# One attention kernel, four edits: shared reciprocals, norms and low parts on GpSimd, one copy

## The chip, the cores and the metric

The kernel runs on one core of a Trainium2 chip. The metric is the device time of one launch in microseconds (us). Before the change it is 1409.32 us, the median of three runs (1409.03 to 1409.68). The engines are called as in the profile: PE is TensorE, DVE is VectorE, ACT is ScalarE, POOL is GpSimd, SP is SyncE.

## The reference: what is computed

A two-layer decoder trunk over 512 tokens of width 1024, all in float32. Layer 0 mixes by retention and an mLSTM; layer 1 by sparse attention. Each layer then has a gated MLP with a short convolution and adds a gated per-layer embedding. The change touches layer 1's mixer alone:

```
z = rms_norm(h) @ w_in                      # q (16 heads x 64), six k/v parts, 48 gates
q = rms_norm(q per head) * 1/8              # 2 groups of 8 heads
kc, vc = compress(k), compress(v)           # 31 blocks: gelu(blk @ w1) @ w2; kc is normed
o_cmp = softmax(q kc) vc                    # compressed branch
o_slc = softmax(q ks) vs                    # "selected": all 8 blocks are selected, so causal
o_win = softmax(q kw) vw                    # window of 512 = all tokens, so causal
o = g0*o_cmp + g1*o_slc + g2*o_win ; y = o @ w_out
```

The two causal branches (here 0 and 1) share the query and differ in keys, values and gate.

## The kernel before

Every float32 product is made of three matmuls: each operand is split in a high part (rounded by ACT, `split` L133) and a low part (the rest, L134), and `mm3` (L150 to L154) adds high x high, high x low and low x high. A weight tile of 128x1024 is fetched, split and kept in one of three buffers by `load` (L136). Which engine makes the low part, DVE or POOL, is told by `lo_seq`, a string that `load` turns round by one letter at each call; `nsa_mixer` (L615) sets it to "v" (DVE) at L951, to "g" (POOL) at L990 and to "v" again at L1050.

Instructions are not issued in the order of the program text. A planner (the Tile framework) sets each engine's order before the run, from priorities and its own costs; loads get a priority 500 instructions ahead of their place. On the chip each engine then goes through its list strictly in order and waits on semaphores.

Layer 1 has two stages of interest.

*The run-up* (about 650 to 770 us). `thin` makes the compressed-branch inputs and gates, `kv` projects keys and values (four tiles of weights), `kv_evac` and `key_stack` norm and transpose them, `hidden` runs the two compressing MLPs (four tiles of w1 each, 32 short matmuls), `q0` and `q1` project the queries of the two groups (four tiles each). These are 22 loads. `q_copy` takes the queries out of PSUM, `q_norm` (L814) norms the first group's four token tiles in two calls: squares L818, sums of squares L819, an inverse root by small instructions L183 to L188, the scaling L825, the split L830 and L831. `q_stack` (L835) transposes. `cmp_keys_t` (L790) transposes the compressed keys' two halves into one PSUM bank, and after each of the two an ACT copy (L795) takes it out. `cmp_scores` and `cmp_probs` make the compressed branch's softmax.

*The loop* (about 770 to 970 us). It has 96 steps: 16 heads times six units in `UNITS` (L34). A unit is a query tile j and one or both branches: (3, branch 0), (3, branch 1), (1, both), (2, branch 0), (2, branch 1), (0, both). `scores` (L887) of a step makes the scores in PSUM (L894 to L896), their negated maximum on DVE (L897), exponentials with row sums on ACT (L899), the reciprocal of the sums on DVE (L900), and on POOL the product of exponentials, reciprocal and gate (L902). Four steps later (`LAG`) `probs` transposes the result on PE (L914) and splits it (L133, L134); `values` (L918) multiplies by the values (L936). The second group's preparation is hung in by step number (`START`, L35, and `hooks`): the embedding's projection from step 1, the second group's `q_norm` at steps 14 and 21, its `q_stack` at 28, 32, 36 and 40, the first group's `cmp_probs` at step 0, the second's `cmp_scores` at 42. `load` uses POOL in this stage: seven tiles.

Of the kernel before, what the change touches and what calls it, by code (L numbers as in the profile page):

```python
# [10 lines left out]
F32 = mybir.dt.float32  # L11
# [3 lines left out]
AF = mybir.ActivationFunctionType  # L15
ALU = mybir.AluOpType
# [3 lines left out]
P = 128  # L20
# [11 lines left out]
WARM = 10  # L32
LAG, VALUES_LAG = 4, 2
UNITS = ((3, (0,)), (3, (1,)), (1, (0, 1)), (2, (0,)), (2, (1,)), (0, (0, 1)))  # L34
START = {"embed": (1, 1), "q_norm": (14, 7), "q_stack": (28, 4), "cmp_scores": 42, "cmp_probs": 47, "fetch": 51, "out": (60, 2)}  # L35
BANKS = {"a": 4, "b": 3, "o": 1}
AHEAD = 500

# [22 lines left out]
class Trunk:  # L61
# [553 lines left out]
    def nsa_mixer(self):  # L615
        nc, I, tc = self.nc, self.I, self.tc
# [3 lines left out]
        with ExitStack() as ctx:  # L620
            np_ = ctx.enter_context(tc.tile_pool(name="nsa", bufs=1))
# [17 lines left out]
            n = self.norm_in(C_NSA)  # L639
            gate = np_.tile([P, NTT, 16, 3], F32, name="gate")  # L640
            kc = np_.tile([P, 2, 64], F32R, name="kc")
# [94 lines left out]
            def hidden(which, xs):  # L736
                ph = self.ps("b")
                for c in range(4):
                    hi, lo = self.load(I["w1"][which, c])
                    for q in range(4):  # L740
                        jj = 4 * c + q
                        ws = slice(256 * q, 256 * q + 256)
                        x = xs[c // 2][:, jj % 8]
                        if jj:
                            nc.tensor.matmul(ph[0:64, 0:256], x[:, 0], lo[:, ws], start=False, stop=False)
                        nc.tensor.matmul(ph[:, 0:256], x.rearrange("p a s -> p (a s)"), hi[:, ws], start=jj == 0, stop=jj == 15)
                        if jj == 0:
                            nc.tensor.matmul(ph[0:64, 0:256], x[:, 0], lo[:, ws], start=False, stop=False)
                hid = self.sc()
                nc.scalar.activation(hid[0:64, 0:256], ph[64:128, 0:256], AF.Copy)  # L750
                nc.vector.tensor_tensor(hid[0:64, 0:256], hid[0:64, 0:256], ph[0:64, 0:256], ALU.add)
                nc.scalar.activation(hid[0:64, 0:256], hid[0:64, 0:256], AF.Gelu_apprx_tanh)
                return hid
# [36 lines left out]
            def cmp_keys_t(st):  # L790
                pk = self.ps("b")
                for a in range(2):
                    src = st[:, 1 - a : 3 - a].bitcast(F32).rearrange("p a d -> p (a d)")
                    nc.tensor.transpose(pk[:, 64 * a : 64 * a + 64], src, self.ident[0:64, 0:64])
                    nc.scalar.activation(kc[:, a], pk[:, 64 * a : 64 * a + 64], AF.Copy)  # L795


            def cmp_values(po):
# [9 lines left out]
            def q_copy(ps, t0):  # L808
                both = self.slot(2 + t0 // 2)
                for i in range(2):  # L810
                    nc.scalar.activation(both[:, i], ps[i], AF.Copy, scale=n.r[:, t0 + i : t0 + i + 1])
                return both

            def q_norm(both, sts):  # L814
                ss = self.small(16)
                for i in range(2):
                    sq = self.sc()
                    nc.vector.tensor_tensor(sq, both[:, i], both[:, i], ALU.mult)  # L818
                    nc.vector.tensor_reduce(ss[:, 8 * i : 8 * i + 8], sq.rearrange("p (h d) -> p h d", h=8), AX, ALU.add)  # L819
                nc.vector.tensor_scalar(ss, ss, 1.0 / 64, EPS, ALU.mult, ALU.add)  # L820
                r = self.rsqrt(ss, 16)
                nc.vector.tensor_scalar(r, r, 0.125, None, ALU.mult)
                for i in range(2):
                    z = both[:, i].rearrange("p (h d) -> p h d", h=8)
                    nc.vector.tensor_tensor(z, z, r[:, 8 * i : 8 * i + 8].unsqueeze(2).to_broadcast([P, 8, 64]), ALU.mult)  # L825
                    halves = []
                    for c in range(2):
                        st = self.y().rearrange("p (h a d) -> p h a d", h=4, a=2)
                        zc = z[:, 4 * c : 4 * c + 4]
                        nc.scalar.activation(st[:, :, 0], zc, AF.Copy)  # L830
                        nc.vector.tensor_tensor(st[:, :, 1], zc, st[:, :, 0].bitcast(F32), ALU.subtract)  # L831
                        halves.append(st)
                    sts.append(halves)
# [40 lines left out]
            def cmp_probs(es):  # L874
                pc = []
                for b in range(2):
                    pt = self.ps("b")
                    for j in range(NTT):
                        c0 = 256 * (j % 2) + P * b
                        nc.tensor.transpose(pt[:, j * P : (j + 1) * P], es[j // 2][:, c0 : c0 + P], self.ident)  # L880
                    hi, lo = self.y(), self.y()
                    self.split(hi, lo, pt)
                    pc.append((hi, lo))
                return pc


            def scores(hd, j, bs):  # L887
                g, nb = hd // 8, len(bs)
                w = (j + 1) * P
                qt, br = qs[hd][:, j * P : w], slice(bs[0], bs[-1] + 1)  # L890
                nmx, sm = [np_.tile([P, nb], F32, name=self.nm("sm"), tag=f"sm{nb}", bufs=4) for _ in range(2)]
                pr = np_.tile([P, T], F32, name=self.nm("pr"), tag="pr", bufs=6)[:, 0 : nb * w].rearrange("p (b s) -> p b s", b=nb)
                s = self.ps("a")[:, 0 : nb * w].rearrange("p (b s) -> p b s", b=nb)
                nc.tensor.matmul(s, qt, kst[0][g][:, br, 0:w], start=True, stop=False)  # L894
                nc.tensor.matmul(s, qt, kst[1][g][:, br, 0:w], start=False, stop=False)  # L895
                nc.tensor.matmul(s[:, :, j * P : w], identb, maskb.unsqueeze(1).to_broadcast([P, nb, P]), start=False, stop=True)  # L896
                nc.vector.tensor_reduce(nmx, s, AX, ALU.max, negate=True)  # L897
                for b in range(nb):
                    nc.scalar.activation(pr[:, b], s[:, b], AF.Exp, bias=nmx[:, b : b + 1], accum_out=sm[:, b : b + 1])  # L899
                nc.vector.reciprocal(sm, sm)  # L900
                for b in range(nb):
                    nc.gpsimd.tensor_scalar(pr[:, b], pr[:, b], sm[:, b : b + 1], gate[:, j, hd, 1 + bs[b] : 2 + bs[b]], ALU.mult, ALU.mult)  # L902
                return pr

            def probs(hd, j, bs, pr):
# [42 lines left out]
                    outs[g][0].append(hi)  # L948
                    outs[g][1].append(lo)

            self.lo_seq = "v"  # L951
            w2r = self.sc()
            nc.sync.dma_start(w2r[:, 0:256], I["w2"])
            w2 = np_.tile([P, 2, 256], F32R, name="w2")
# [19 lines left out]
            st = cmp_keys(po)  # L974
            sts = []
            zq = [q_copy(q0.ps[0:2], 0), q_copy(q0.ps[2:4], 2)]
            q_norm(zq[0], sts)
            q_norm(zq[1], sts)
            hv = hidden(1, xv)
            q1 = self.Tokens(self, I["w_q"][1], n)  # L980
            q1.steps(0, 2)
# [9 lines left out]
            sts1 = []  # L991
            zq = [q_copy(q1.ps[0:2], 0), q_copy(q1.ps[2:4], 2)]
# [5 lines left out]
            def piece(half, m):  # L998
                return lambda: self.out_piece(I["w_nso"], half, m, *outs[half])
# [3 lines left out]
            def embed(m):  # L1003
                return lambda: emb.step(m)

            def more_q(lo, hi):
                def run():
                    for hd in range(lo, hi):
                        qs.append(q_stack(sts1, hd))
                return run  # L1010

            def set_probs(g):
                def run():
                    pcs[g] = cmp_probs(ess[g])
                return run
# [4 lines left out]
            hooks = {}  # L1020

            def at(key, fs):
                first, step = START[key]
                for i, f in enumerate(fs):
                    hooks.setdefault(first + step * i, []).append(f)

            hooks[0] = [set_probs(0)]
            at("embed", [embed(m) for m in range(KD)])
            at("q_stack", [more_q(2 * i, 2 * i + 2) for i in range(4)])
            at("q_norm", [lambda i=i: q_norm(zq[i], sts1) for i in range(2)])  # L1030
            hooks.setdefault(START["cmp_scores"], []).append(set_scores)
            hooks.setdefault(START["cmp_probs"], []).append(set_probs(1))
            hooks.setdefault(START["fetch"], []).append(lambda: self.fetch(self.keep, (0, 2)))
            at("out", [piece(0, m) for m in range(KD)])

            for step in range(len(seq) + LAG + VALUES_LAG + 2):
                if step < len(seq):
                    live[step] = scores(*seq[step])
                if 0 <= step - LAG < len(seq):
                    hd, j, bs = seq[step - LAG]  # L1040
# [231 lines left out]
```

## Time and profile before

| | us |
|---|---|
| median of three runs | 1409.32 |
| the profiled execution's own time | 1410.24 |
| its span, first to last instruction | 1408.5 |
| PE busy | 1378.5 (98%) |
| DVE busy | 852.0 (60%) |
| ACT busy | 640.1 (45%) |
| POOL busy | 349.7 (25%) |
| mean granted TensorE clock | 0.991 |

Busy time is the time in which an engine had an instruction in work. Idle time in brackets behind an instruction is that of its engine just before, with what ended it.

### The profile page before, as it was taken

What the parts mean: (1) busy time and instruction counts of PE and PEld (TensorE: products, weight loads), DVE (VectorE), ACT (ScalarE), POOL (GpSimd) and SP (SyncE); (2) the same over time, 40 slices, a digit from 0 to 9 for tenths busy, and PEclk for the clock granted to TensorE, in tenths of its full rate; (3) what the DMA queues carried; (4) which work ended last, traced back from release to release, by engine and by line L of the source; (5) the groups of instructions that cost most, each with busy time, mean ns of one, the idle gap of its engine ahead of it and who ended that gap; (6) DMA issues with size and microseconds to landing.
All of it is one profiled execution on the core that took longest, in us unless ns stands there. A gap on an engine that the chain in (4) does not pass through costs nothing.

```text
span 1408.5 us, 18029 instructions
## 1 busy us (share of the span) xinstructions
PE 1378.5 (98%) x6726; PEld 1130.2 (80%) x6726; DVE 852.0 (60%) x1419; ACT 640.1 (45%) x1122; POOL 349.7 (25%) x342
## 2 busy tenths in 40 slices
PE   9999999999999999999998989999999999999998
PEld 7778778888888888887787757787888888888887
DVE  6665656565346435566857798777565437534555
ACT  5257426443224313454554777777444224323342
POOL 3465102122041001122112645544222013100120
PEclk9999999999999999999998999999999999999999
DMA  6433323233223332333442100010233323333232
GB/s 216 128 113 95 106 77 111 86 101 103 92 90 105 91 104 83 97 124 95 131 143 63 46 1 31 16 46 17 75 105 105 92 88 105 99 96 96 83 107 75
DMA packets 40031, 127.96 MB, mean 91 GB/s; under 512 B 4740, under 2 KB 5380, under 8 KB 39944
## 3 DMA queue, kind: packets, MB, share of 16 engines
q1 hardware_dynamic: 39656, 126.68, 29.2%
q8 instruction: 53, 0.87, 0.3%
q14 instruction: 34, 0.28, 0.1%
q10 hardware_dynamic: 288, 0.14, 0.0%
HBM read 122.60 MB, written 3.15 MB: 89 GB/s over the span
## 4 chain that ended last, share of the span: by engine, by line
PE 83%; DVE 5%; issue 4%; ACT 3%; POOL 1%; DMA 0%; ACTq 0%; POOLq 0%; DVEq 0%
PE ps L152 25%; PE ps L153 25%; PE ps L154 25%; PE ps L914 2%; PE ps L936 2%; DVE pt L134 1%; DVE sm L897 1%; PE ps L894 1%; ACT pr L899 1%; PE ps L895 1%; PE ps L363 1%; ACT pt L133 1%; ACT wh L133 1%; PE ps L421 1%; POOL acc L200 1%
## 5 line engine op out<-in xcount | busy, mean ns | idle before, releaser
L152 PE MATMUL ps<-y,wh 128*128 128x512 f32 (+1 forms) x1112 | 435.3, 392 | 1.8 <-ACT rb L239 1.1
L153 PE MATMUL ps<-y,wh 128*128 128x512 f32 (+1 forms) x1112 | 432.5, 389 | 0.6 <-POOL y L134 0.6
L154 PE MATMUL ps<-y,wl 128*128 128x512 f32 (+1 forms) x1112 | 432.0, 389 | 0.0
L133 ACT ACTIVATE wh<-wr 128x1024 fp32r<-128x1024 f32 (+2 forms) x223 | 230.2, 1036 | 420.5 <-PE ps L153 347.3
L134 DVE TENSOR_TENSOR wl<-wr,wh 128x1024 fp32r<-128x1024 f32 (+2 forms) x196 | 239.9, 1226 | 43.8 <-ACT wh L133 43.1
L152 PEld LDWEIGHTS ps<-y,wh 128*128 128x128 f32 x1112 | 209.3, 188 | 45.5 <-ACT rb L239 1.3
L154 PEld LDWEIGHTS ps<-y,wl 128*128 128x128 f32 x1112 | 209.3, 188 | 43.5 <-DVE wl L134 0.2
L153 PEld LDWEIGHTS ps<-y,wh 128*128 128x128 f32 x1112 | 209.4, 188 | 43.2 <-POOL y L134 1.1
L1075 POOL TENSOR_TENSOR sc<-sc,rb 128x512 f32<-128x512 f32 x44 | 56.8, 1291 | 476.5 <-ACT sc L1074 476.5
L200 POOL TENSOR_TENSOR acc<-acc,sc 128x512 f32<-128x512 f32 x48 | 73.6, 1534 | 257.9 <-ACT sc L198 255.0
L153 PE MATMUL ps<-gl,wh 128*128 128x512 f32 x352 | 137.1, 389 | 0.0
L154 PE MATMUL ps<-gh,wl 128*128 128x512 f32 x352 | 137.0, 389 | 0.0
L152 PE MATMUL ps<-gh,wh 128*128 128x512 f32 x352 | 137.0, 389 | 0.0
L1090 DVE TENSOR_TENSOR hp<-hp,ps 128x512 f32<-128x512 f32 x48 | 33.0, 688 | 130.4 <-PE ps L154 130.4
L902 POOL TENSOR_SCALAR pr<-pr,sm,gate 128x512 f32<-128x512 f32 (+3 forms) x128 | 79.3, 625 | 85.5 <-DVE sm L900 45.1
L134 POOL TENSOR_TENSOR wl<-wr,wh 128x1024 fp32r<-128x1024 f32 x25 | 61.2, 2451 | 111.0 <-ACT wh L133 103.7
L1076 DVE TENSOR_TENSOR sc<-ps,sc 128x512 f32<-128x512 f32 x44 | 30.4, 692 | 92.4 <-POOL sc L1075 83.2
L1068 DVE TENSOR_TENSOR a<-ps,rb 128x512 f32<-128x512 f32 x44 | 30.4, 690 | 92.1 <-PE ps L154 89.3
L153 PEld LDWEIGHTS ps<-gl,wh 128*128 128x128 f32 x352 | 66.1, 188 | 13.7
L152 PEld LDWEIGHTS ps<-gh,wh 128*128 128x128 f32 x352 | 66.1, 188 | 13.7
L154 PEld LDWEIGHTS ps<-gh,wl 128*128 128x128 f32 x352 | 66.1, 188 | 13.7
L1074 ACT ACTIVATE sc<-sc 128x512 f32<-128x512 f32 x44 | 27.8, 632 | 101.1 <-DVE sc L1073 101.1
(282 smaller groups left out, 2033.0 us busy)
## 6 DMA issues: line engine op xcount, KB each, us to landing
wr<-in_w_up_dram SPq DMA_DIRECT2D x88, 512.0 KB, 3.6
wr<-in_w_down_dram SPq DMA_DIRECT2D x32, 512.0 KB, 3.5
wr<-in_w_plg_dram SPq DMA_DIRECT2D x16, 512.0 KB, 3.6
wr<-in_w_down_dram SPq DMA_DIRECT2D x16, 384.0 KB, 3.1
hp<-in_xT_dram SPq DMA_DIRECT2D x16, 256.0 KB, 4.0
wr<-in_w_abo_dram SPq DMA_DIRECT2D x8, 512.0 KB, 3.7
wr<-in_w_dram SPq DMA_DIRECT2D x8, 512.0 KB, 3.9
wr<-in_w_q_dram SPq DMA_DIRECT2D x8, 512.0 KB, 4.0
```

Source lines behind the costliest of these rows:

```text
L133: self.nc.scalar.activation(hi, src, AF.Copy)
L134: (eng or self.nc.vector).tensor_tensor(lo, src, hi.bitcast(F32), ALU.subtract)
L152: mm(out, ah, bh, start=first, stop=False)
L153: mm(out, ah, bl, start=False, stop=False)
L154: mm(out, al, bh, start=False, stop=last)
L200: eng.tensor_tensor(n.acc, n.acc, sq, ALU.add)
L902: nc.gpsimd.tensor_scalar(pr[:, b], pr[:, b], sm[:, b : b + 1], gate[:, j, hd, 1 + bs[b] : 2 + bs[b]], ALU.mult, ALU.mult)
L914: nc.tensor.transpose(pb[:, i * P : (i + 1) * P], pr[:, n, i * P : (i + 1) * P], self.ident)
L1068: nc.vector.tensor_tensor(a, pa, n.b, ALU.mult)
L1075: nc.gpsimd.tensor_tensor(c, c, n.b, ALU.mult)
L1076: nc.vector.tensor_tensor(c, pb, c, ALU.mult)
L1090: nc.vector.tensor_tensor(self.h[m], self.h[m], ps, ALU.add)
```

## The change

The reciprocals of the row sums: `scores` now keeps one 128x2 tile of sums per head and query tile. Where the two branches are two steps (j = 3 and 2), the second step inverts both sums at once and then issues both POOL products. The maxima get buffers of their own. The squares L818 and scalings L825 of the second group's `q_norm` go from DVE to POOL, at steps 6 and 14 in place of 14 and 21; `q_stack` goes to 20, 26, 32 and 38; the first group's `cmp_probs` to step 3. In the run-up the low parts alternate, DVE and POOL: 11 of the 22 go to POOL. In `cmp_keys_t` one ACT copy follows both transposes.

```diff
-START = {"embed": (1, 1), "q_norm": (14, 7), "q_stack": (28, 4), "cmp_scores": 42, ...}
+START = {"embed": (1, 1), "q_norm": (6, 8), "q_stack": (20, 6), "cmp_scores": 42, ...}
@@ cmp_keys_t
                     nc.tensor.transpose(pk[:, 64 * a : 64 * a + 64], src, self.ident[0:64, 0:64])
-                    nc.scalar.activation(kc[:, a], pk[:, 64 * a : 64 * a + 64], AF.Copy)
+                nc.scalar.activation(kc.rearrange("p a n -> p (a n)"), pk[:, 0:P], AF.Copy)
@@ q_norm
-            def q_norm(both, sts):
+            def q_norm(both, sts, eng):
-                    nc.vector.tensor_tensor(sq, both[:, i], both[:, i], ALU.mult)
+                    eng.tensor_tensor(sq, both[:, i], both[:, i], ALU.mult)
-                    nc.vector.tensor_tensor(z, z, r[:, 8 * i : 8 * i + 8].unsqueeze(2).to_broadcast([P, 8, 64]), ALU.mult)
+                    eng.tensor_tensor(z, z, r[:, 8 * i : 8 * i + 8].unsqueeze(2).to_broadcast([P, 8, 64]), ALU.mult)
@@ scores
+            parts = []
-                nmx, sm = [np_.tile([P, nb], F32, name=self.nm("sm"), tag=f"sm{nb}", bufs=4) for _ in range(2)]
+                nmx = np_.tile([P, nb], F32, name=self.nm("nmx"), tag=f"sm{nb}", bufs=4)
+                if bs[0] == 0:
+                    parts.append([np_.tile([P, 2], F32, name=self.nm("sm"), tag="sums", bufs=4), []])
+                sm, prs = parts[-1]
...
                 for b in range(nb):
-                    nc.scalar.activation(pr[:, b], s[:, b], AF.Exp, bias=nmx[:, b : b + 1], accum_out=sm[:, b : b + 1])
-                nc.vector.reciprocal(sm, sm)
-                for b in range(nb):
-                    nc.gpsimd.tensor_scalar(pr[:, b], pr[:, b], sm[:, b : b + 1], gate[:, j, hd, 1 + bs[b] : 2 + bs[b]], ALU.mult, ALU.mult)
+                    nc.scalar.activation(pr[:, b], s[:, b], AF.Exp, bias=nmx[:, b : b + 1], accum_out=sm[:, bs[b] : bs[b] + 1])
+                    prs.append(pr[:, b])
+                if bs[-1] == 1:
+                    nc.vector.reciprocal(sm, sm)
+                    for b in range(2):
+                        nc.gpsimd.tensor_scalar(prs[b], prs[b], sm[:, b : b + 1], gate[:, j, hd, 1 + b : 2 + b], ALU.mult, ALU.mult)
@@ the run-up's head, the first group's norms, the hooks
-            self.lo_seq = "v"
+            self.lo_seq = "vg"
-            q_norm(zq[0], sts)
-            q_norm(zq[1], sts)
+            q_norm(zq[0], sts, nc.vector)
+            q_norm(zq[1], sts, nc.vector)
-            hooks[0] = [set_probs(0)]
+            hooks[3] = [set_probs(0)]
-            at("q_norm", [lambda i=i: q_norm(zq[i], sts1) for i in range(2)])
+            at("q_norm", [lambda i=i: q_norm(zq[i], sts1, nc.gpsimd) for i in range(2)])
```

## Rows read from the trace of the kernel before

**Rows 1.** Windows: start:end, length, busy us of each engine, granted clock, DMA.
```profile
660.00:740.00 80.00, 78.88 (x397) 64.00 (x398) 56.32 (x112) 40.24 (x67) 14.46 (x20) 1.00 0.41 127
740.00:756.00 16.00, 11.61 (x56) 8.51 (x54) 14.82 (x45) 7.46 (x17) 5.08 (x2) 1.00 0.28 75
756.00:763.00 7.00, 7.00 (x28) 6.24 (x27) 2.63 (x6) 1.62 (x4) 0.00 (x0) 0.51 0.15 57
...
777.00:800.00 23.00, 21.01 (x130) 16.71 (x129) 13.60 (x34) 18.16 (x47) 14.73 (x18) 1.00 0.09 27
800.00:850.00 50.00, 43.37 (x282) 32.32 (x282) 46.96 (x134) 37.59 (x118) 26.46 (x35) 0.97 0.06 20
...
890.00:940.00 50.00, 49.97 (x314) 40.66 (x314) 36.87 (x86) 33.41 (x93) 21.98 (x31) 1.00 0.11 33
940.00:970.00 30.00, 29.55 (x227) 24.40 (x225) 26.59 (x71) 27.82 (x88) 18.85 (x30) 1.00 0.06 19
```
**Rows 2.** Waits of PE, 650 to 1000 us: total us, times, longest.
```profile
PE ps L914 <- DVE pt L134: 3.8, 8, 0.9
PE ps L880 <- POOL sc L870: 2.6, 3, 1.3
PE ps L894 <- ACT pr L899: 2.6, 5, 1.4
PE ps L838 <- DVE y L831: 2.1, 2, 1.9
PE ps L794 <- ACT kc L795: 2.0, 1, 2.0
```
**Rows 3.** Timeline, end of the run-up: start us, us, instruction, [idle before].
```profile
742.70 3.49 DVE L825 TENSOR_TENSOR ep<-ep,tiny 128x512 f32<-128x512 f32 x2
...
742.93 2.71 POOL L134 TENSOR_TENSOR wl<-wr,wh 128x1024 fp32r<-128x1024 f32 x1 [27.72 <-ACT wh L133]
...
747.25 0.27 PE L794 MATMUL ps<-ident,stc 64*128 64x64 f32 x1 [1.97 <-ACT kc L795]
...
750.75 0.75 DVE L831 TENSOR_TENSOR y<-ep,y 128x256 fp32r<-128x256 f32 x2
...
752.02 2.36 POOL L134 TENSOR_TENSOR wl<-wr,wh 128x1024 fp32r<-128x1024 f32 x1 [6.38 <-ACT wh L133]
...
752.28 2.72 DVE L831 TENSOR_TENSOR y<-ep,y 128x256 fp32r<-128x256 f32 x2 [0.77 <-ACT y L830]
...
754.71 0.44 PE L838 MATMUL ps<-ident,y 128*128 128x128 f32 x2 [1.89 <-DVE y L831]
```
**Rows 4.** Groups on DVE, 660 to 770 us: count, busy us, mean ns, idle before.
```profile
L134 DVE TENSOR_TENSOR wl<-wr,wh 128x1024 fp32r<-128x1024 f32 x20 | 24.6, 1241 | 12.3 <-ACT wh L133 12.1
```
**Rows 5.** Groups on POOL, 770 to 972 us.
```profile
L134 POOL TENSOR_TENSOR wl<-wr,wh 128x1024 fp32r<-128x1024 f32 x4 | 9.6, 2395 | 1.2 <-ACT wh L133 1.2
...
L862 POOL TENSOR_TENSOR sc<-sc,tiny 128x512 f32<-128x512 f32 x4 | 4.2, 1048 | 9.1 <-DVE tiny L861 7.3 <-DVE tiny L867 1.8
```
**Rows 6.** Timeline, last w1 tile of the first compressing MLP.
```profile
696.71 2.35 DVE L134 TENSOR_TENSOR wl<-wr,wh 128x1024 fp32r<-128x1024 f32 x2
...
697.98 0.34 PE L745 MATMUL ps<-wl,pt 128*64 128x256 f32 x1 [0.18 <-DVE wl L134]
```
**Rows 7.** Groups on DVE, 800 to 850 us.
```profile
L818 DVE TENSOR_TENSOR sc<-ep 128x512 f32<-128x512 f32 x4 | 3.5, 884 | 0.0
...
L825 DVE TENSOR_TENSOR ep<-ep,tiny 128x512 f32<-128x512 f32 x4 | 2.8, 750 | 0.0
...
L900 DVE RECIPROCAL sm<-sm 128x1 f32<-128x1 f32 x16 | 2.5, 154 | 0.4 <-ACT pr L899 0.4
```
**Rows 8.** Timeline of POOL: the two products of one pair of branches at j = 3.
```profile
953.89 0.77 POOL L902 TENSOR_SCALAR pr<-pr,sm,gate 128x512 f32<-128x512 f32 x1 [0.79 <-DVE sm L900]
...
956.25 0.77 POOL L902 TENSOR_SCALAR pr<-pr,sm,gate 128x512 f32<-128x512 f32 x1 [1.58 <-DVE pt L134]
```
**Rows 9.** Timeline of PE: the transposes of the first of these.
```profile
955.50 0.60 PE L914 MATMUL ps<-ident,pr 128*128 128x128 f32 x4
```

More of the change, by code (lines that the diff above doesn't have):

```diff
@@ L34 @@
 UNITS = ((3, (0,)), (3, (1,)), (1, (0, 1)), (2, (0,)), (2, (1,)), (0, (0, 1)))
-START = {"embed": (1, 1), "q_norm": (14, 7), "q_stack": (28, 4), "cmp_scores": 42, "cmp_probs": 47, "fetch": 51, "out": (60, 2)}
+START = {"embed": (1, 1), "q_norm": (6, 8), "q_stack": (20, 6), "cmp_scores": 42, "cmp_probs": 47, "fetch": 51, "out": (60, 2)}
 BANKS = {"a": 4, "b": 3, "o": 1}
```

## The prediction

> **What bounds the kernel now.** PE is busy for 98% of the span, so only stretches in which it idles or runs at the lower clock can pay. I looked for them in the busy times by windows first. The windows of layer 1 show four of them [rows 1]. From 660 to 740 us PE idles 80.00 - 78.88 = 1.1 us: the run-up is bound by PE. From 740 to 756 it idles 4.4 of 16 us, and DVE is busy for 14.82 of them. From 756 to 763 it never idles, but the granted clock is 0.51, near 1.2 GHz, after the engine had stood still; at 2.4 GHz the same work takes 7 x 0.51 = 3.6 us, so 3.4 us go there. From 777 to 800 it idles 2.0 us. From 800 to 850 it idles 6.6 us at a clock of 0.97 (1.5 us more), with DVE busy for 46.96 of 50 us. From 890 to 940 it idles for 0.03 us: the second half of the loop is bound by PE again, and what is saved on other engines there is worth nothing.
>
> Then the waits of PE, to see what ends last in each [rows 2]. In the loop it is DVE's low parts before transposes (3.8 us) and exponentials (2.6). The transposes L880 of the compressed probabilities wait for POOL's L870 (2.6 us in three waits; two of them, 1.7 us together at 779 and 782, are the first group's). L838 waits 2.1 us for DVE's L831, and the second transpose of L794 waits 2.0 us for one ACT copy.
>
> Last the timeline around these two [rows 3]. POOL makes a low part from 742.93 to 745.64, and the two scalings L825 on DVE, started at 742.70, last 3.49 us; they take 1.5 us elsewhere (2 x 750 ns) [rows 7]. POOL makes another from 752.02 to 754.38, and two L831 last 2.72 us where two took 0.75 just before. So a DVE instruction with both inputs in SBUF stands still while POOL works. The ACT queue waits behind DVE's L825 for its inputs, the key copy behind that, PE behind the copy: 1.97 us. L838 waits 1.89 us for the second.
>
> **The change, part by part.** The terms are against the profiled execution, 1410.24 us; the median of the runs is 0.92 lower.
>
> *One copy of the keys.* PE makes both transposes without waiting, so the wait of 1.97 us goes. What is late next is L838, which waits for DVE's L831, not for PE: if PE arrives 1.97 us sooner and DVE does not, the wait just moves there. Ends: nothing, and both waits (-3.9). I take the middle: -2.0.
>
> *Low parts on POOL in the run-up.* DVE loses 11 instructions of 1.24 us, 13.6 us [rows 4]; POOL gets 11 of 2.4 us, 26 us [rows 5], and has room: 14.46 of 80 us busy [rows 1]. No DMA is added. Three buffers of weights hide a longer low part where a tile feeds PE for several us. They don't in the compressing MLPs: their last tile's low part is the first of the two from 696.71, and PE, already idle for 0.18 us, starts on it at 697.98 [rows 6]. Every fourth w1 tile becomes POOL's: 2.4 - 1.2 = 1.2 us later, less some 0.6 by which POOL can start sooner, since DVE has other work before it; two MLPs, +1.2. Then the standstill [rows 3]: the second and fourth tile of q1 fall on 732 to 742 us, where DVE works toward L831 with instructions that have both inputs in SBUF. Each takes 1.2 us from DVE and may hold it for 2.4, so it costs up to 1.2 or gains up to 1.2; I take +1.3 for both. Behind a held instruction stands all of DVE's queue, and behind that L830 on ACT and L838 on PE. Ends: -2.5 (DVE's freed time counts in full and nothing is held) and +4.8 (1.2 + 2.4, and 1.2 for a tile of kv that falls on the small instructions of the first norm). Taken: +2.5, on the side of the row that shows the hold.
>
> *The stretch at 1.2 GHz* from 756 to 763 follows on those two waits. Without them it can go (-3.4), with one longer wait it stays (0). Taken: half, -1.7.
>
> *Second group's norms.* In the stage from 800 to 850 us DVE loses the four squares and four scalings, 3.5 + 2.8 = 6.3 us, and half of 16 reciprocals of 154 ns, 1.2 us [rows 7]: 46.96 becomes 39.4 of 50, 79% [rows 1]. At 74% (890 to 940) PE idles 0.03 of 50 us, at 89% (940 to 970) 0.45 of 30. The first of the two calls moves to before 800 with all that it has on DVE, where DVE has 13.60 of 23 us. I leave 1.8 of the 6.6 us: -4.8. Ends: -6.6 and 0 (if latency, not DVE's load, is what makes the waits). The lower clock in this stage goes with the waits: -1.5, ends -1.5 and 0.
>
> *What POOL pays for them.* Eight instructions of at least 1.05 us, by the one of the same shape with a spread operand (L862) [rows 5]. The first call's four (4.2 us) come to 786 to 805 us, where POOL also has three low parts of 2.4 us: in 777 to 800 it goes from 14.73 to 18.9 of 23 us. Behind them in POOL's queue stand the products L902, and behind those PE's transposes. Ends: 0 (they fall in gaps) and +4.2 (all four stand ahead of a product that PE wants). Taken: +1.5, since DVE's relief makes the products ready sooner.
>
> *Sums inverted together.* It saves 32 of 96 reciprocals, 4.9 us of DVE; after 890 us that is worth nothing. It adds a wait: the product of a pair's first branch now waits for the second's exponentials. One pair shows it: the first product ends at 954.66 and the second at 957.02 [rows 8]; PE begins the first's transposes behind 955.50 [rows 9]. Paired, the first can end at 957.0, 1.4 us late. The same comparison over all 32 pairs finds 11 late, by 0.4 to 1.4 us; five lie between 800 and 850 us, where DVE's relief covers them, six later, together 6.0 us. There PE's queue holds other work whose order can change. Ends: 0 and +6.0; taken: +1.5. The separate buffers of maxima and sums loosen a wait of DVE for POOL that the stage does not show (its groups idle 0.0 to 0.4 us) [rows 7]: 0.
>
> *First `cmp_probs` at step 3.* The 1.7 us for L870 lose to matmuls of later steps: -1.3, ends -1.7 and 0. `q_stack` only moves its copies, two each for DVE and ACT a call; it ends at step 38 in place of 40: 0.
>
> Sum: -2.0 + 2.5 - 1.7 - 4.8 - 1.5 + 1.5 + 1.5 - 1.3 = -5.8 us; 1410.24 - 5.8 - 0.92 = 1403.5 us. The low ends give -19.6, the high ends +15.0.
>
> **The rivals.**
>
> *POOL holds DVE in the run-up (slower).* Place: 728 to 756 us. For it speaks the hold [rows 3], against it that PE lost only 1.1 us in 80 before and that DVE has idle time in front of its low parts (12.3 us over 20) [rows 4]. The key wait returns at L838 (0 in place of -2.0), the low parts cost their high end, +4.8, and a second stretch at 1.2 GHz follows, +3.4: +8.2. The loop's terms (-4.8 - 1.5 + 1.5 + 1.5 - 1.3 = -4.6) stay: +3.6, 1412.9 us. It decides once the run-up costs over 7.4 us. The Trainium skill (GPSIMD Engine Reference, section Specifications) says that POOL shares its SBUF interfaces with DVE and gets in the way of DVE instructions with two SBUF inputs; by that rule, with which the 2.72 us beside 0.75 agree, each low part moved to POOL takes more of DVE's time than it gives back wherever DVE has such work.
>
> *POOL's queue and the pairing eat the gain (no change).* The norms stand ahead of products (+4.2), late pairs cost 4.5: -2.0 + 2.5 - 1.7 - 4.8 - 1.5 + 4.2 + 4.5 - 1.3 = -0.1: 1409.2 us. For it: PE begins transposes about a microsecond after a product ends [rows 8, 9]. Against: POOL is busy for half of 800 to 850.
>
> *All stalls go (faster by more).* Keys -3.9, clock -3.4 and -1.5, DVE stage -6.0, `cmp_probs` -1.3; low parts, queue and pairs together +2.5: -13.6, so 1395.7 us. For it: DVE loses 13.6 us before 750 and its queue is the last cause of both waits there. Against it the hold itself [rows 3].
>
> **How the numbers follow.** Forecast 0.45, with a range of its own from 1400.5 to 1406.5; held run-up 0.20; gain eaten 0.22; all stalls gone 0.13. About 0.2% (2.8 us) is what a measurement of this kernel can tell from no change. Faster by more than that: 0.45 + 0.13 less 0.02 of the forecast's upper end, 0.56. Within it: 0.02 + 0.22 less 0.02, 0.22. Slower: 0.20 + 0.02, 0.22. The range for 8 in 10 goes from the third rival's time to a little over the first's: 1395 to 1413.5 us.
>
> **What would show it.** Right: PE's wait for L795 gone and L838's at most 2 us; no 1.2 GHz between 750 and 763; PE idle under 3 us in the first 50 us of full heads, DVE there under 85%. Wrong: L838 or L745 waiting for low parts with DVE instructions of 2 us and more beside POOL's (first rival); PE waiting for L902 at the first transposes of a pair (second). A run-up that starts its loop over 3 us later than before, or PE's idle time in the loop unchanged, would make the forecast wrong.

## The result and the profile after

The changed kernel takes 1416.84 us, the median of five runs (1414.41 to 1417.31). Its ratio to the kernel before is 1.0051, with a 95% interval of 1.0036 to 1.0065: slower by about 7 us. The forecast was 1403.5 us, faster, and the time lies above its range. The profiled execution took 1416.84 us with a span of 1415.1.

First the windows of the changed kernel, cut as in [rows 1]: start:end, length, busy us of PE, weight loads, DVE, ACT and POOL, granted clock, DMA.

```profile
660.00:740.00 80.00, 69.65 (x320) 55.39 (x320) 43.45 (x79) 33.46 (x59) 31.48 (x27) 0.94 0.32 96
...
756.00:763.00 7.00, 6.33 (x30) 4.86 (x29) 6.86 (x31) 2.82 (x7) 1.85 (x2) 1.00 0.38 129
763.00:777.00 14.00, 10.59 (x49) 9.36 (x48) 8.28 (x20) 5.15 (x12) 3.25 (x2) 0.76 0.24 75
```

From 660 to 740 us PE now idles 80.00 - 69.65 = 10.4 us where it idled 1.1 [rows 1]. DVE did get its relief there (56.32 to 43.45 us) and POOL its load (14.46 to 31.48), and yet the stretch that PE bounded before is the one that loses.

Two windows of each kernel, cut where PE issues the loop's second scores and where it ends the last transposes, divide the loss from the gain. First before, then after.

```profile
600.00:771.85 171.85, 165.68 (x801) 135.32 (x800) 121.22 (x235) 84.10 (x136) 35.24 (x43) 0.97 0.37 114
771.85:972.73 200.88, 188.24 (x1236) 149.17 (x1236) 164.87 (x425) 151.11 (x440) 104.92 (x147) 0.97 0.08 25
```

```profile
600.00:785.70 185.70, 168.73 (x801) 137.87 (x800) 120.91 (x223) 83.57 (x135) 62.95 (x55) 0.95 0.34 104
785.70:978.93 193.23, 181.09 (x1236) 144.56 (x1236) 159.03 (x387) 149.48 (x440) 109.90 (x153) 0.99 0.09 27
```

The run-up is 185.70 - 171.85 = 13.9 us longer: PE's idle time in it grows from 6.2 to 17.0 us (10.8), and its mean clock falls from 0.97 to 0.95. The loop is 200.88 - 193.23 = 7.7 us shorter. What comes behind is the same (436 us in both). 13.9 - 7.7 = 6.2, against 6.6 between the two spans. Some of both is the clock: PE is at 1.2 GHz for 9.0 us of the first window and 11.5 of the second before, for 17.1 and 3.4 after. That is the same 20.5 us in all, 8.1 of them moved, which at half speed are worth up to 4.1 us of the loss and as much of the gain.

The waits of PE in the changed kernel, 600 to 1000 us, answer to [rows 2]: total us, times, longest.

```profile
PE ps L153 <- POOL wl L134: 4.5, 1, 4.5
PE ps L152 <- ACT y L133: 3.3, 1, 3.3
PE ps L921 <- POOL pr L909: 3.1, 4, 1.5
PE ps L921 <- DVE pt L134: 2.8, 4, 2.0
PE ps L745 <- POOL wl L134: 2.8, 2, 1.7
PE ps L152 <- ACT y L206: 2.2, 1, 2.2
PE ps L234 <- DVE tiny L188: 2.2, 1, 2.2
```

Two kinds of wait are new in the run-up (the lines of L921 are the loop's). In one PE waits for a low part that POOL makes: 4.5 and 2.8 us, so 7.3 of the 10.8 us by which its idle time grew. In the other it waits for a chain through DVE (3.3, 2.2 and 2.2 us). Of these the 2.2 us for L206 were 0.6 before and the 2.2 for L188 nothing; the 3.3 stand where the waits for L795 and L831, 3.9 us together, stood [rows 3]. The timeline shows what stands behind each. The lines are start us, us, instruction, [idle before].

The last gated embedding of layer 0, while POOL makes the low part of 650.03 to 652.43 us, and PE at its end:

```profile
650.03 2.40 POOL L134 TENSOR_TENSOR wl<-wr,wh 128x1024 fp32r<-128x1024 f32 x1 [36.70 <-ACT wh L133]
...
650.50 2.48 DVE L1156 SCALAR_TENSOR_TENSOR sc<-ep,cols,sc 128x512 f32<-128x512 f32 x1 [0.74 <-ACT sc L1155]
...
661.67 0.50 PE L152 MATMUL ps<-y,wh 128*128 128x512 f32 x1 [2.22 <-ACT y L206]
```

The first norm of layer 1, all engines:

```profile
669.05 2.40 POOL L134 TENSOR_TENSOR wl<-wr,wh 128x1024 fp32r<-128x1024 f32 x1 [3.99 <-ACT wh L133]
...
669.13 2.35 DVE L183 TENSOR_SCALAR tiny<-tiny 128x4 int32<-128x4 int32 x1
...
673.51 0.65 PE L234 MATMUL ps<-ident,tiny 128*128 128x128 f32 x4 [2.21 <-DVE tiny L188]
```

The end of the run-up:

```profile
754.02 2.35 DVE L186 TENSOR_TENSOR tiny<-tiny 64x1 f32<-64x1 f32 x1
...
761.51 2.39 POOL L134 TENSOR_TENSOR wl<-wr,wh 128x1024 fp32r<-128x1024 f32 x1 [5.15 <-ACT wh L133]
761.59 2.34 DVE L186 TENSOR_TENSOR tiny<-tiny 128x16 f32<-128x16 f32 x1
...
765.95 1.33 ACT L830 ACTIVATE y<-ep 128x256 fp32r<-128x256 f32 x4 [4.22 <-DVE ep L825]
...
767.82 0.42 PE L152 MATMUL ps<-w,y 128*128 128x64 f32 x1 [3.32 <-ACT y L133]
```

L1156 takes 0.74 us when POOL is idle, L183 0.16. Beside POOL's low part L183 ends with it and L1156 0.6 us after it. Eight DVE instructions between 640 and 786 us are held so, for 16.0 us together (their time less the shortest of the same line and shape in any run). Seven, 13.9 us, are beside low parts that the change moved. The eighth is the L186 of 761.59, beside the first of the loop's low parts, which POOL made before the change too; in the kernel before, the loop's first two held two instructions for 4.2 us [rows 3]. What moved freed 11 x 1.24 = 13.6 us of DVE [rows 4]. But L1156 and L183 stand in the chains of the two waits of 2.2 us, and the L186 of 754.02 and of 761.59 in that of the 3.3, since DVE's queue has no gap from the first of them to the L825 in front of L830. For low parts on DVE PE had waited only 0.4 us in all before.

POOL's own queue where the keys are normed, and PE behind it at the second tile of the first group's queries:

```profile
708.59 5.23 POOL L701 TENSOR_TENSOR sc<-sc,gains 128x128 f32<-128x128 f32 x8 [4.48 <-DVE sc L699]
713.79 2.33 POOL L134 TENSOR_TENSOR wl<-wr,wh 128x1024 fp32r<-128x1024 f32 x1
```

```profile
716.18 0.80 PE L153 MATMUL ps<-wl,y 128*128 128x512 f32 x1 [4.50 <-POOL wl L134]
```

A low part stands behind eight of POOL's own gains (L701), and PE waits 4.50 us for it, the longest wait of the run-up. The granted clock falls to 1.2 GHz three times before the loop, at 674.61, 715.57 and 766.77 us, each time around one of PE's long stops (those that end at 673.51, 716.18 and 767.82).

### The profile page after: what moved, and what is told of

The parts are those of the page before. It is cut to its first block, busy times and chain, and to the rows that moved or that the text cites. A ratio compares the mean times of both kernels' runs of the same rounds, so it can differ in the third digit from the quotient of the medians.

```text
span 1415.1 us, 17986 instructions
## 1 busy us (share of the span) xinstructions
PE 1374.4 (97%) x6726; PEld 1127.8 (80%) x6726; DVE 847.2 (60%) x1368; ACT 637.9 (45%) x1121; POOL 383.2 (27%) x361
## 4 chain that ended last, share of the span: by engine, by line
PE 82%; DVE 7%; ACT 3%; issue 3%; POOL 2%; POOLq 0%; ACTq 0%; DVEq 0%
PE ps L153 25%; PE ps L152 25%; PE ps L154 25%; PE ps L921 2%; PE ps L943 2%; ACT pr L904 1%; PE ps L363 1%; ACT pt L133 1%; DVE nmx L902 1%; DVE wl L134 1%; PE ps L900 1%; PE ps L899 1%; DVE pt L134 1%; PE ps L421 1%; DVE tiny L186 1%
## 5 line engine op out<-in xcount | busy, mean ns | idle before, releaser
L134 DVE TENSOR_TENSOR wl<-wr,wh 128x1024 fp32r<-128x1024 f32 (+2 forms) x185 | 226.8, 1228 | 48.3 <-ACT wh L133 47.8
L134 POOL TENSOR_TENSOR wl<-wr,wh 128x1024 fp32r<-128x1024 f32 x36 | 88.1, 2449 | 160.9 <-ACT wh L133 140.5
L909 POOL TENSOR_SCALAR pr<-pr,sm,gate 128x512 f32<-128x512 f32 (+3 forms) x128 | 77.3, 615 | 65.5 <-DVE sm L907 45.8
L154 PEld LDWEIGHTS ps<-gh,wl 128*128 128x128 f32 x352 | 66.1, 188 | 13.6
```

The costliest lines, as they stand in the source:

```text
L134: (eng or self.nc.vector).tensor_tensor(lo, src, hi.bitcast(F32), ALU.subtract)
L154: mm(out, al, bh, start=False, stop=last)
L909: nc.gpsimd.tensor_scalar(prs[b], prs[b], sm[:, b : b + 1], gate[:, j, hd, 1 + b : 2 + b], ALU.mult, ALU.mult)
```

## The experiments

The main theory (A): the run-up's low parts on POOL cost about 14 us, and the edits to the loop gain about 7, independently. The first rival (B): the loop only looks quicker because it starts late, with its loads long there, so that without the loss there is no gain. Two readings of the loss came next: POOL's work *holds* DVE, or the low parts wait in POOL's *queue*. Ratios are this kernel's time over that of the kernel before, measured beside it, with 95% intervals.

**e1: the change without its low parts.**

```diff
-            self.lo_seq = "vg"
+            self.lo_seq = "v"
```

> The changed kernel with the run-up's low parts all on DVE again, the rest kept. Theory A (the low parts on POOL alone make it slower: they hold DVE and stand in POOL's own queue, so the loop's first scores come 14.8 us late, and the other edits gain in the loop): the first scores come back to 764 to 768 us, the loop from first to last scores stays near 189.5 us (201.0 before), 1416.8 - 14 = 1402 to 1404 us. Theory B (the loop is only shorter because it starts late, with weights, norms and POOL's work already in hand): the first scores come back, the loop goes back to about 199 to 201 us, 1406 to 1410 us.

Measured: 0.9952 (0.9936 to 0.9969), 1400.57 us, a little under A's range. The rest of the change gains 6.8 us. The first scores come back to 765.32 us, as both theories have it. From first to last scores the loop takes 191.5 us, near A's 189.5 and far from B's 199 to 201; cut as above it takes 195.24, 5.6 less than before where the changed kernel gained 7.7. The clock can make that difference: e1's loop is at 1.2 GHz for 10.2 us, the changed kernel's for 3.4.

**e2: the kernel before with the low parts of the change alone.**

```diff
-            self.lo_seq = "v"
+            self.lo_seq = "vg"
```

> The kernel before with only the alternation of low parts between DVE and POOL in the run-up. Theory A: the first scores come at 778 to 783 us as in the changed kernel, the loop stays near 201 us, 1421 to 1425 us. Theory B: the first scores come late all the same, but the loop is 8 us shorter or more, 1412 to 1417 us.

Measured: 1.0102 (1.0087 to 1.0117). The second scores come at 783.46 us, 11.6 later than before, and the loop takes 200.91 us from there, as before (200.88). The two parts add up: 1.0051 / 0.9952 = 1.0099. A holds, B falls: the loop is no shorter for starting late (e2), and shorter with an undisturbed start (e1).

**e3: e1 with the sums inverted step by step, as before the change.** The body of `scores` is that of the kernel before.

> The changed kernel with low parts on DVE in the run-up and each step's sums inverted by themselves again, as before. By the prediction's term (the pairing makes products late by 0.4 to 1.4 us, and costs 1.5 us net) it is 0 to 3 us faster than with paired sums; if DVE's 32 fewer reciprocals count more, up to 3 us slower.

Measured: 0.9943 (0.9930 to 0.9956). 1.3 us faster than e1, but the intervals overlap: undecided here, taken up again in e9.

**e4: e1 with the second group's squares and scalings on DVE, at the new steps.**

```diff
-            at("q_norm", [lambda i=i: q_norm(zq[i], sts1, nc.gpsimd) for i in range(2)])
+            at("q_norm", [lambda i=i: q_norm(zq[i], sts1, nc.vector) for i in range(2)])
```

> The changed kernel with low parts on DVE in the run-up and the second group's squares and scalings on DVE, at the new steps 6 and 14. If DVE's load in 800 to 850 us is what made PE wait, as the prediction had it, 3 to 6 us slower than with them on POOL; if calling them earlier is what counts, within 2 us of it.

Measured: 0.9969 (0.9960 to 0.9978), 0.0017 above e1: POOL in place of DVE is worth some 2.4 us, with intervals that overlap. It lies between the two readings, within 2 us and 3 to 6, and decides for neither.

**e5: the hold by itself.** The kernel before, every low part on DVE, and POOL makes 11 subtractions of the same shape into a tile that nobody reads.

```diff
-            self.lo_seq = "v"
+            self.lo_seq = "vd"
+            self.idle = np_.tile([P, 1024], BF16, name="idle")
...
@@ load
...
+                if kind == "d":
+                    nc.gpsimd.tensor_tensor(self.idle, hi.bitcast(F32), hi.bitcast(F32), ALU.subtract)
```

> The kernel before, all low parts on DVE; beside every second one of the run-up POOL subtracts the tile's high part from itself into a spare tile (bfloat16), which nobody reads. 11 POOL instructions of about 2.4 us with no reader. Theory 'hold' (DVE instructions with two SBUF inputs stand still while POOL works): the second step's scores come 5 to 9 us later than the 771.9 of before, 1413 to 1417 us. Theory 'queue' (what costs is that PE and DVE wait for POOL's own late results): within 2 us of 771.9, 1407 to 1410 us.

Measured: 1.0123 (1.0110 to 1.0136): 17 us, more than expected, and the second scores come at 785.48 us, 13.6 later than before, not 5 to 9. No low part of the run-up waits in POOL's queue here. DVE (L1153 and L186 are the L1156 and L183 of the changed kernel):

```profile
650.34 2.38 DVE L1153 SCALAR_TENSOR_TENSOR sc<-ep,cols,sc 128x512 f32<-128x512 f32 x1
...
668.87 1.85 DVE L186 TENSOR_SCALAR tiny<-tiny 128x4 int32<-128x4 int32 x1
```

Twelve instructions of DVE are held for 20.4 us together, ten of them, 16.2 us, beside the idle operations and two beside the loop's first two low parts, as before the change. PE's waits in the run-up, 600 to 790 us, are of the changed kernel's kind, but all except 1.1 us (for POOL's L711) for DVE or ACT:

```profile
PE ps L717 <- DVE st L710: 3.8, 1, 3.8
PE ps L748 <- DVE wl L134: 3.0, 3, 1.5
PE ps L155 <- ACT y L209: 2.8, 1, 2.8
...
PE ps L717 <- POOL st L711: 1.1, 1, 1.1
```

So work on POOL stops DVE though nobody reads its result, and a queue of late low parts falls as the only cause. What e5 does not give is the hold's share of e2: it leaves DVE the 13.6 us of low parts, and its idle operations also stand in front of POOL's other work.

**e6: the queue.** e2 with POOL's own instructions of the key and value norms on DVE.

```diff
-                    nc.gpsimd.tensor_tensor(sq, kk, kk, ALU.mult)
+                    nc.vector.tensor_tensor(sq, kk, kk, ALU.mult)
...
-                nc.gpsimd.tensor_copy(st[:, :, :, 0], st[:, :, :, 2])
+                nc.vector.tensor_copy(st[:, :, :, 0], st[:, :, :, 2])
```

(and the gains L701 likewise)

> The kernel before with alternating low parts in the run-up (as in the run of the low parts alone, 1421.8 us), and the keys' squares, gains and copies (L690, L701, L708) moved from POOL to DVE, so that no low part stands behind them in POOL's queue. 'Queue': PE's wait of 4.5 us for a POOL low part near 715 us and most of the rest go, second scores at 772 to 776 us (783.5 in that run), 1410 to 1414 us. 'Hold': that wait shrinks, but DVE is still held 11 times and has some 4 us more to do; second scores at 778 to 783, 1416 to 1421 us.

Measured: 1.0054 (1.0041 to 1.0067), 1415.10 us, 0.0048 or 6.7 us under e2. The second scores come at 777.12 us. Both lie between the ranges of the two theories. The wait of 4.5 us is gone from the list of PE's waits, 600 to 780 us; the two chains and the MLPs' low parts stay, with the same lengths as in the changed kernel:

```profile
PE ps L745 <- POOL wl L134: 2.8, 2, 1.7
PE ps L152 <- ACT y L206: 2.2, 1, 2.2
PE ps L234 <- DVE tiny L188: 2.2, 1, 2.2
```

Just under half of e2's loss goes when the keys' instructions do not stand in POOL's queue; the rest does not need them. The split is rough: DVE has the keys' work on top here, and is held for 20.4 us where e2 has 16.1.

**e7: the hold, taken out where it stood before.** e3 with the first two low parts of the loop's loads (at 743 and 752 us in [rows 3]) on DVE.

```diff
-            self.lo_seq = "g"
+            self.lo_seq = "vvggggg"
```

> The run with sums apart (low parts of the run-up on DVE, 1398.7 us), and also the loop's first two low parts, which fall at 742 to 754 us beside the first group's norms, on DVE. 'Hold': the two waits of PE for L831 (2.2 and 1.9 us) shrink to 1 us or less together, 1393 to 1396 us. If DVE's own load makes them, DVE has 2.5 us more to do there: they stay, 1398 to 1401 us.

Measured: 0.9902 (0.9889 to 0.9915), 1394.05 us: faster than both kernels, and 0.0041 or 5.8 us under e3. PE's waits for L831, 4.8 us in e3, are 0.8, as "hold" has it. DVE's queue:

```profile
746.89 1.29 DVE L825 TENSOR_TENSOR ep<-ep,tiny 128x512 f32<-128x512 f32 x2
748.11 1.22 DVE L134 TENSOR_TENSOR wl<-wr,wh 128x1024 fp32r<-128x1024 f32 x1
749.24 1.42 DVE L831 TENSOR_TENSOR y<-ep,y 128x256 fp32r<-128x256 f32 x4
```

The scalings L825, 3.49 us in [rows 3], take 1.29; four L831 take 1.42 where two took 2.72. The low part that was kept away from DVE to spare it 1.22 us had cost it more than 2. The granted clock is 1.00 from 600 us to the end of the loop.

**e8: e1 with `q_norm` and `q_stack` at the steps of the kernel before (14, 7 and 28, 4), the norms on POOL.**

> The changed kernel with low parts on DVE in the run-up, and the second group's norms and stacks at their old steps (14 and 21; 28, 32, 36, 40), norms on POOL. If it was DVE's load that counted, whatever the step, within 1.5 us of the same kernel at the new steps (1400.6 us). If calling them earlier is what counts, 2 to 5 us slower, 1402.5 to 1405.5.

Measured: 0.9976 (0.9966 to 0.9986), 0.0024 above e1: the earlier steps are worth some 3.4 us, in the second reading's range, again with intervals that just overlap.

**e9: e7 with the sums paired**, that is the changed kernel with the run-up's low parts and the loop's first two on DVE.

> The changed kernel with all low parts of the run-up and the first two of the loop on DVE, the sums paired as in the change; e7 is the same with the sums inverted step by step (0.9902 of the kernel before). It settles what the pairing does once the run-up leaves no stretch at 1.2 GHz to blur it. Theory P (the wait added by the pairing costs, since a first branch's product ends up to 1.4 us later): slower than e7 by 1.5 to 4 us, ratio 0.991 to 0.993. Theory Q (PE's queue holds other work, the pairing is free): within 1 us of e7, ratio 0.9895 to 0.991. Theory R (the reciprocals saved on DVE pay): under 0.9895.

Measured: 0.9898 (0.9881 to 0.9915), 1393.63 us, 0.0004 under e7. The pairing costs and gains nothing that shows: -0.6 us here and +1.3 by e3 against e1, each uncertain by some 3 us. The ratio lies in Q's band; its interval does not exclude the nearest parts of the other two. The waits that the prediction feared do come: PE waits for a paired product (L909) for 2.9 us in four waits here and in e1, for 1.2 in one (L902) in e7 and e3. They do not show in the time.

**e10: the kernel before with nothing but the two low parts of e7.**

> The kernel before with the loop's first two low parts (at 743 and 752 us) on DVE and nothing else. Theory H (a POOL low part holds DVE, and the two waits of PE at 747 and 754 and the 1.2 GHz behind them come from that): both waits and the half-speed stretches at 756 and 770 go, the loop begins 5 to 9 us earlier, ratio 0.9935 to 0.997. Theory L (it is latency of the chain through DVE, ACT and PE, and e7 gained because the change had cut it): waits stay, ratio 0.998 to 1.000.

Measured: 0.9950 (0.9935 to 0.9965), so 7 us from one string. No wait of PE for L795 or L831 above 0.3 us is left, and the second scores come at 762.62 us in place of 771.85. The window up to them, against the 171.85 us at 0.97 before:

```profile
600.00:762.62 162.62, 160.19 (x797) 130.84 (x796) 118.47 (x236) 83.88 (x136) 28.56 (x39) 1.00 0.37 118
```

PE idles 2.4 us in it (6.2 before), and none of it is at 1.2 GHz. H holds. 0.9902 / 0.9950 = 0.9952: the loop's edits, with the sums apart, give here what they give with the sums paired in e1.

**e11: the kernel before with the one copy of the keys alone.**

```diff
-                    nc.scalar.activation(kc[:, a], pk[:, 64 * a : 64 * a + 64], AF.Copy)
+                nc.scalar.activation(kc.rearrange("p a n -> p (a n)"), pk[:, 0:P], AF.Copy)
```

> The kernel before with the one copy of the compressed keys and nothing else. Theory M (the wait just moves to L838, which waits for DVE's L831): the wait for L795 is under 0.5 us, L838 waits 3.5 to 4.2 us in all, ratio 0.999 to 1.001. Theory K (the prediction's middle, -2.0 us): one wait of about 1.9 us left, ratio 0.9975 to 0.999.

Measured: 1.0001 (0.9992 to 1.0010). The waits of PE, 600 to 1000 us, and the two places on the timeline:

```profile
PE ps L838 <- DVE y L831: 3.8, 3, 2.2
```

```profile
741.01 3.50 DVE L825 TENSOR_TENSOR ep<-ep,tiny 128x512 f32<-128x512 f32 x2
...
749.54 0.44 PE L838 MATMUL ps<-ident,y 128*128 128x128 f32 x2 [2.19 <-DVE y L831]
...
750.59 2.73 DVE L831 TENSOR_TENSOR y<-ep,y 128x256 fp32r<-128x256 f32 x2 [0.77 <-ACT y L830]
...
753.04 0.69 PE L838 MATMUL ps<-ident,y 128*128 128x128 f32 x2 [1.44 <-DVE y L831]
```

The wait for L795 is gone. In place of 1.97 us there and 1.89 at L838 [rows 3], PE waits 2.19 and 1.44 us at L838, behind the same held L825 and the same held L831. M holds.

The costs of the parts, as shares of the kernel before (0.0010 is 1.4 us):

| part | from | ratio | us |
|---|---|---|---|
| low parts of the run-up on POOL | e2; after / e1 | +0.0102; +0.0099 | +14 |
| one copy of the keys | e11 | +0.0001 | 0 |
| norms on POOL, not DVE | e1 to e4 | -0.0017 | -2.4 |
| `q_norm`, `q_stack` earlier | e1 to e8 | -0.0024 | -3.4 |
| sums paired | e9 to e7; e1 to e3 | -0.0004; +0.0009 | 0 (-0.6; +1.3) |
| all but the low parts | e1 | -0.0048 | -6.8 |

A difference of two runs' ratios is uncertain by some 0.002 (3 us), so that the norms on POOL and the pairing are not clear of nothing by themselves, and the earlier steps barely are. The first `cmp_probs` at step 3 has no run of its own.

## Why the prediction was wrong

**The step that failed: "Low parts on POOL in the run-up", taken at +2.5 us with ends of -2.5 and +4.8; measured, about +14.** The prediction had one mechanism, the hold, saw it in [rows 3] and gave the rival built on it 0.20. Slower, as this rival had it, is what happened, but not where it looked and not by the hold alone: it named 728 to 756 us, where PE waits 1.7 us in the changed kernel, for a low part, and just under half of the loss goes with POOL's queue (e6), which neither the term nor the rival had. How much of the rest is the hold and how much the slower low part itself, no run separates. The price was too small at four points.

- *Where the hold strikes.* The prediction looked for it at q1's tiles alone, and there two instructions are held for 4.3 us; PE's next wait behind them is 0.7 us (at 758.40, 0.4 before), and the second of them is in the chain of the 3.3 us at 767.82. The timeline after shows it from POOL's first low part on: in the embedding's chain at 650 us (PE waits 2.22 us at 661.67 for the L206 at its end, where it waited 0.6 before), and in the first norm at 669 us (2.21 us). The norm was in the high end as 1.2 us, the embedding not at all. Both places could be looked up in the trace before, as DVE instructions between 645 and 770 us whose result PE wants soon; but L183, the one held in the norm, has a single input, which [rows 3] do not warn of.
- *What the hold takes.* The prediction weighed 1.2 us freed against up to 2.4 held, as if it were one account. The freed time lay in slack (12.3 us of idle time stood in front of the 20 low parts of [rows 4]), the held time in part in the chain. The clock's price came on top, up to 4.1 us before the loop.
- *POOL's queue.* "And has room: 14.46 of 80 us busy" was an average over the stretch. At 708.59 us eight gains stand in POOL's queue for 5.23 us, and a low part behind them is 4.50 us late for PE. It belongs to a tile of the queries, which feeds PE for several us; that the three buffers hide a longer low part at such tiles did not hold here. The prediction named what stands behind a slow POOL instruction in the loop, but not in the run-up; e6 prices it at 6.7 us, clock included.
- *The MLPs' low parts.* Priced at +1.2 for both, they cost PE 2.8 us (1.13 and 1.66).

The rival's arithmetic gave the run-up +8.2 and the total 1412.9; the run-up lost 13.9, and the loop came out better than -4.6 (-7.7 in the window, clock included), so the time was 1416.84.

**One copy of the keys**: -2.0 taken, 0 measured (e11). Its own sentence, "the wait just moves there", was the answer. Both waits hang on DVE's queue with its two held instructions, and PE, which arrived sooner at L838 in e11, waited there instead. e10 takes the cause away, and both go. The signs given for it came in the changed kernel (L795's wait gone, L838's 0.4 us), but say nothing for the term: with the run-up otherwise as before, in e1, L838 waits 4.4 us.

**The stretch at 1.2 GHz**: half of it taken, -1.7. Neither happened as forecast: from 756 to 763 us the clock is 1.00, but three such stretches stand elsewhere in the run-up. In e1, where the rest of the run-up is as before, 10.2 us at 1.2 GHz stay, and the waits stay. They go only with the hold (e7, e10). The term also left one out: between the lines of [rows 1] lie 763 to 777 us, where the kernel before is at 1.2 GHz from 769.72 to 776.54 us; in e10 that stretch goes too.

**The loop**: -4.6 taken (-4.8 - 1.5 + 1.5 + 1.5 - 1.3), -6.8 measured in e1, right in direction and somewhat small. Norms and their earlier steps, -4.8 by the terms (-4.8 - 1.5 + 1.5), are -5.8 if e4's and e8's differences may be added, which no run with both undone shows. The pairing was priced at +1.5 for six late pairs of up to 6.0 us: some of the waits come, nothing shows in the time (e9). The wait for L870 went from 2.6 us in three waits [rows 2] to 2.0 in two in e1, not by 1.3. But the sign that the prediction gave for its loop did not come: it wanted PE idle for under 3 us and DVE under 85% in the first 50 us. In the changed kernel PE idles 6.1 us there and DVE is at 87%:

```profile
785.00:835.00 50.00, 43.87 (x275) 34.04 (x275) 43.65 (x115) 37.68 (x106) 34.73 (x41) 0.97 0.13 41
```

Over the whole loop the idle time hardly moves, 12.6 to 12.1 us. The gain lies in PE's busy time, 188.2 to 181.1 us for the same 1236 instructions. Up to 4.1 of these 7.1 us are the clock (11.5 us at 1.2 GHz before, 3.4 after). The other 3 us are not settled. In e1 nearly the same time as before is spent at 1.2 GHz (10.2 us), and the busy time still falls by 4.4. That DVE's load made stalls of PE, the reason given for -4.8, is therefore not shown; that the loop's edits gain together is (e1, and e7 against e10).

## What to carry to other kernels

Before work is given to POOL, look at what DVE does beside it: if that has two inputs in SBUF and a chain waits for it, the move can cost more than it frees. The same look at two low parts that POOL already made found 7 us in the kernel before (e10). Judge an idle engine's room in the microseconds where the new work arrives, with what stands ahead of it in its queue, and not as a busy share over a stage. Where two waits in a row hang on the same late queue, removing the first alone can be worth nothing (e11).

## What the runs showed of the hardware

Beside a POOL low part of 2.4 us, DVE's instructions with two tensor inputs in SBUF were held, down to the smallest (L186 of 64x1, 2.35 us for 0.14), and two with a single input too (L183, int32 128x4, 2.35 for 0.16; L693, f32 128x16, 1.87 for 0.17). Not held were the same L183 of 64x1 (0.13), reductions from SBUF (L691, 0.42 us beside POOL and elsewhere), instructions with an input from PSUM (`pt` L134 of 128x512, 0.69 for 0.67) and a reciprocal of 128x2 (0.17).

The hold goes both ways, which the prediction did not have. POOL's timeline of the changed kernel, and then POOL's and DVE's of e6:

```profile
753.25 3.11 POOL L134 TENSOR_TENSOR wl<-wr,wh 128x1024 fp32r<-128x1024 f32 x1 [3.54 <-ACT wh L133]
```

```profile
712.60 4.46 POOL L134 TENSOR_TENSOR wl<-wr,wh 128x1024 fp32r<-128x1024 f32 x1 [2.25 <-ACT wh L133]
...
713.04 0.69 DVE L701 TENSOR_TENSOR sc<-sc,gains 128x128 f32<-128x128 f32 x3
713.65 0.75 DVE L707 TENSOR_TENSOR st<-sc,st 128x256 fp32r<-128x256 f32 x2
714.32 0.49 DVE L708 CAST st<-st 128x256 fp32r<-128x256 f32 x2
```

The first fits a wait for a DVE low part that ran from 752.89 to 754.10 us, and then 2.26 us of its own. The second fits a wait of 2.2 us for a train of DVE instructions that ended at 714.81, and 2.25 from there. So POOL also waited for instructions of the train that began after its own start at 712.60. The Trainium skill (SBUF — State Buffer, section "SBUF: two separate sides") calls the pair of ports that the two share "an **exclusive lock**, not a bandwidth split"; the trace agrees, with 0.85 us of 3.11 spent waiting.
